# A decoder layer on one core: first transfers in halves on two queues, queries copied out of PSUM at once, values in two halves, the last factors by Ln and Exp, one result by TensorE

## The chip, the cores and the metric

The kernel runs on one core of a Trainium2 chip. The metric is the device time of one execution in microseconds (us), as the median of several runs. Engines: TensorE (PE; its weight loads are PEld in the profile), VectorE (DVE), ScalarE (ACT), GpSimd (POOL) and SyncE (SP). Transfers are issued from the queues of SP and ACT.

## The reference

One layer over 256 tokens of width 2048, batch 1, in float32. `rms_norm` has a learned gain.

```python
h = rms_norm(x, mix_pre_norm)
y = hybrid_mixer(h, ...)               # mLSTM and RWKV-7 mixers side by side, gated merge
x = x + rms_norm(y, mix_post_norm)
h, m = rms_norm(x, xattn_pre_norm), rms_norm(mem, mem_norm)
# cross_attention(h, m): 4 heads of 128, 256 memory tokens
q, (k, v) = h @ wq, split(m @ wkv)
p = softmax(q k^T / sqrt(128));  o = p v;  y = o @ wo
x = x + rms_norm(y, xattn_post_norm)
h = rms_norm(x, ffn_pre_norm)
u = conv_b + sum_j conv_w[j] * shift(h @ w_up, 2 - j)     # three taps along the tokens
gate, up = split(u)                                       # 8192 columns each
x = x + rms_norm((gelu(gate) * up) @ w_down, ffn_post_norm)
```

## The kernel before

**Products.** All big products run over pairs of numbers: each float32 operand is split into a high part, rounded to the `fp32r` format, and a low part (the rest, in the same format). One product is three matmuls: high by high, low by high, high by low. A weight chunk comes by a transfer (`raw`, three buffers; the first block's eight chunks lie in `wsm`), ACT casts it to the high part (`wh`, L361) and DVE subtracts to get the low part (`wl`, L382); both have four buffers, so the cast of chunk i waits until PE has finished chunk i - 4. `Feed` keeps this: `dma(i)`, `hi(i)`, `lo(i)` make sure that chunk i is on its way, cast, or complete.

**Blocks.** `run` takes a list of weight blocks in a fixed order. Kind `fm` gives features by tokens, kind `tm` tokens by features. A block sums over k in two or four PSUM banks (`acc` or `aux`, four of each). A block's `tail` of n means that its last n chunks are converted first, and that the products of these chunks then run bank by bank instead of chunk by chunk, so that the banks end one after another. When a block is done, its `evac` generator is given to the planner.

**The planner.** `Spread` (`side`) hands out the side work in pieces (one `next` of a generator) at each `half`, which `run` calls twice for each two-row chunk and after every second row of a tail. Each engine has a credit: a half adds 600 to DVE's and 820 to ACT's, both capped at 1200, and a piece takes what `Meter` counts for its instructions (ACT 200 + 0.83 for each element of a partition, DVE 70 + 1.04; casts and splits of the weights aren't counted, nor is work issued outside a piece). A piece of the list `bulk` goes only while both credits are above 0; the generators of the list `chains` go, in the order in which they were added, if both are above -700. `need(task)` issues pieces at once until the task is done. All this fixes the order of instructions on each engine's queue while the program is built; on the chip each engine works through its queue in order and waits on semaphores.

**The start.** x comes as eight pieces of two feature tiles (`x_load`, SP), alternating with the chunks of the first block (`w_sm`), all on SP's queue; ACT's queue takes the parameters `par` (columns 0 to 15, the first gains, and then the other 173). `pre_sm` lets PE run 8 warm-up products (`keep_warm`, 16 instructions), and `first` converts chunk 0 and x tiles 0 and 1: DVE casts the chunk's first half, ACT the second; ACT makes `hh` = x times gain (high), DVE `hl` (low).

**Cross-attention.** The order is: keys (`w_xk`), the first two of eight value chunks (`w_xv`, block `xv`), queries (`w_xq`, block `xq_`), the other six value chunks, of which the last two are the tail, and the output projection (`w_xo`). While the queries' block runs, `Residual` adds the mixer's result to x, and its statistics (`stx`) are closed by `column_of_sums` (a fold on DVE, a product `st` on PE, a power on POOL). `qx_evac` copies the queries out of PSUM (`qT`) and adds the chain of the four softmax heads, `stagger`: its first piece issues the first head's scores (`xsc`), after which `M["res"].wait(4)` gives up its turn until the statistics are done (four times at most). From then on each piece moves every live head by one stage and brings in the next: stage 1 scores and their maximum `mx`, stage 2 Exp, reciprocal and scaling (`spr`), stage 3 four transposes by PE (`xpT`) and the copy `pT`. `vx_evac` copies the values out of PSUM, scaled by the memory rows' factors (`xv`, four copies on ACT). `xo` multiplies `pT` by the values, heads 0 and 1 and then 2 and 3, and splits the result into `oT` for `w_xo`.

**The end.** The last block (`w_fd`, n = 1) has one row of k to a chunk and 64 rows; its operand `as` is split two rows at a time by `asplit` (ACT high, DVE low; one buffer for even pairs of rows, one for odd), two rows ahead of use. Its four banks are tokens 0 to 127 (banks 0 and 1, t = 0) and 128 to 255 (banks 2 and 3, t = 1). For each bank `squares` sums squares on ACT, `gain` scales on DVE; `finish(t)` gives the factor `rco` (`rstd_of`: sum and scale on DVE, power on POOL), and `result(t, c)` adds to x and issues the output transfer of a 128x512 piece. Reads of one bank by ACT and DVE follow each other.

Of the kernel before, what the change touches and what calls it, by code (L numbers as in the profile page):

```python
# [12 lines left out]
ALU = mybir.AluOpType  # L13
# [132 lines left out]
def _layer(ctx, tc, nc, d, dbg):  # L146
# [21 lines left out]
    def C(name, tag, shape=None, dt=F32):  # L168
        return mp.tile(shape or [P, S], dt, tag=tag, bufs=1, name=name)
# [13 lines left out]
    def keep_warm(n):  # L183

        q = aux("warm", [P, P])
        for _ in range(n):
            mm(q, ones.broadcast_to((P, P)), ones.broadcast_to((P, P)))
# [3 lines left out]
    xq = [x0[c // 4][:, c % 4 * 2:c % 4 * 2 + 2] for c in range(8)]  # L191
    par = cp.tile([P, NPAR], F32, name="par")
    act.dma_start(par[:, 0:16], d["par"][:, 0:16])
    act.dma_start(par[:, 16:NPAR], d["par"][:, 16:NPAR])
    con = cp.tile([P, NCON], F32, name="con")
    up = C("up", "bg0", [P, 1024])

# [9 lines left out]
    pool.memset(mhalf, -0.5)  # L207
    epsc = mhalf[:, 15:16]
    pool.memset(epsc, EPS)
    act.activation(mhalf[:, 0:1], mhalf[:, 0:1], AF.Copy)  # L210
    ones = cp.tile([P, 1], F32, name="ones")
    pool.memset(ones, 1.0)
    bones = cp.tile([P, P], F32R, name="bones")
# [112 lines left out]
    class Feed:  # L326
        def __init__(self, order):
# [3 lines left out]

            self.sm = [big(f"wsm{i}", [P, 4, 2, 384]) for i in range(2)]

        def dma(self, upto):
            while self.nd <= min(upto, len(self.src) - 1):
                s = self.src[self.nd]
                if self.nd < 8:
                    r = self.sm[self.nd // 4][:, self.nd % 4]
                else:
                    r = wp.tile(list(s.shape), F32, tag="raw", bufs=3, name="raw")  # L340
                sp.dma_start(r, s)
                self.raw[self.nd] = r
                self.nd += 1
# [74 lines left out]
    def run():  # L418
        order = visits()
        feed = Feed([(b["kind"], s) for b, c0, c1 in order for s in b["srcs"][c0:c1]])  # L420
        for c in range(8):
            x_load(c)
            feed.dma(c)
        i = 0
        pend, ring = [], []
        for b, c0, c1 in order:
# [63 lines left out]
            if nt:  # L490

                feed.lo(i + nt - 1)
                steps = []
                for s in tail:
                    w = feed.st.pop(i)
                    for kj in range(s.shape[1]):
                        steps.append((w[0][:, kj], w[1][:, kj]) + tuple(b["xs"](k)))
                        k += 1
                    i += 1
                n = len(steps)  # L500
                for g, o in enumerate(banks):
                    if b["kind"] == "tm":
                        for si, (wh, wl, xh, xl) in enumerate(steps):
                            if b is xv:
                                halves(banks, (wh, wl, xh, xl), False, si == n - 1, g)
                            else:
                                tm_products(o, g * P * 512 // b["cols"], g * 512 % b["cols"], (wh, wl, xh, xl), False,
                                            si == n - 1)
                            if si % 2:
                                side.half()  # L510
                    else:
                        turns = [(si, m) for si in range(n) for m in range(2)]
                        if g + 1 == len(banks):
                            turns.sort(key=lambda v: v[1])
                        for ti, (si, m) in enumerate(turns):
                            wh, wl, xh, xl = steps[si]
                            c = slice((g * 2 + m) * P, (g * 2 + m + 1) * P)
                            q = b["apart"] if g and m else o[:, m]
                            mm(q, wh[:, c], xh, start=ti == 0 or (bool(g and m) and si == 0), stop=False)
                            mm(q, wh[:, c], xl, start=False, stop=False)  # L520
                            mm(q, wl[:, c], xh, start=False, stop=si == n - 1)
                            if ti % 4 == 3:
                                side.half()
                    if g == 0:
                        feed.lo(i + 1)
                feed.dma(i + 4)
            if end:
                b["task"] = side.add(b["evac"](banks))
                pend.append(b["task"])

    def W(name, blk):
# [16 lines left out]

    def pre_sm(ci, feed):
        if ci == 0:  # L550
            keep_warm(8)
            feed.first()
            for c in range(1, 3):
                x_piece(c)
                feed.lo(c)
        if ci + 3 < 8:
            x_piece(ci + 3)
        else:

            for c in range((ci - 5) * 2, (ci - 5) * 2 + 2):  # L560
                st0.add(xq[c])
        if ci == 4:
            sp.dma_start(con, d["con"])
# [973 lines left out]
    def qx_evac(ps):  # L1537
# [3 lines left out]
        tasks["sm"] = side.add(stagger([softmax(h) for h in range(4)]), chain=1)  # L1541
        yield

    def vx_evac(ps):
        xv = C("xv", "bg0", [P, 2, 512])
        M["xv"] = [xv[:, t] for t in range(2)]
        for g in range(2):
            for t in range(2):
                act.activation(M["xv"][t][:, g * S:(g + 1) * S], ps[g][:, t], AF.Copy, scale=stm.rc[:, t:t + 1])
        yield  # L1550

    def stagger(gens):
# [50 lines left out]
    def xo():  # L1603
        M["oT"] = U("oT", [P, 2, 4, S], F32R)
        for h2 in range(2):
            q = aux("xo", [P, 2, S])
            for j in range(2):
                h = h2 * 2 + j
                for mt in range(2):
                    mm(q[:, j], M["xv"][mt][:, h * P:(h + 1) * P], M["pT", h][:, mt], start=(mt == 0), stop=(mt == 1))  # L1610
            split(M["oT"][:, 0, h2 * 2:h2 * 2 + 2], M["oT"][:, 1, h2 * 2:h2 * 2 + 2], q)
            yield

# [100 lines left out]
    def ax(n):  # L1714
        def xs(k):
            kk = n * 64 + k
            if kk == 58:
                side.need(fu["task"])
            if kk == 24:
                load_gain()  # L1720
            if k % 2 == 0:
                asplit(kk)
                if kk + 2 < 128 and (k < 62 or n == 0):
                    asplit(kk + 2)
            return M["as"].pop(kk)
        return xs
# [19 lines left out]
    def fd_evac(n):  # L1746

        def gen(ps):
            if n:
                z = mp.tile([P, 2, 1024], F32, tag="hT", bufs=2, name="z3")  # L1750
            else:
                z = U("z3", [P, 2, 1024])
            M["z3", n] = z

            if n == 0:
                M["ssq"], M["rco"] = small("ssq", [P, 2, 4], bufs=1), small("rco", [P, 2], bufs=1)
            ssq, rco = M["ssq"], M["rco"]

            def squares(g):
                jk = T2("jk", [P, 512])  # L1760
                act.activation(jk, ps[g], AF.Square, accum_out=ssq[:, g // 2, n * 2 + g % 2:n * 2 + g % 2 + 1])

            def gain(g):
                c = slice(g % 2 * 512, g % 2 * 512 + 512)
                dve.tensor_mul(z[:, g // 2, c], ps[g], M["gain"][:, n * 1024 + c.start:n * 1024 + c.stop])

            def finish(t):
                ss = small("sso", [P, 1], bufs=2)
                dve.tensor_reduce(ss, ssq[:, t], axis=AX.X, op=ALU.add)
                rstd_of(rco[:, t:t + 1], ss, D)  # L1770

            def result(t, c):
                f = slice(c % 2 * 512, c % 2 * 512 + 512)
                x, z_ = M["xt"][c // 2][:, t, f], M["z3", c // 2][:, t, f]
                if t and c == 1:
                    act.activation(z_, z_, AF.Copy, scale=rco[:, t:t + 1])
                    pool.tensor_add(x, x, z_)
                else:
                    dve.scalar_tensor_tensor(x, z_, rco[:, t:t + 1], x, op0=ALU.mult, op1=ALU.add)
                (act if t and c != 1 else sp).dma_start(d["out"][t, :, c * 512:c * 512 + 512], x)  # L1780

            if n == 0:
                for g in range(4):
                    squares(g)
                    gain(g)
                    yield
                return
            squares(0)
            gain(0)
            squares(1)  # L1790
            finish(0)
            gain(1)
            squares(2)
            result(0, 0)
            result(0, 1)
            gain(2)
            result(0, 2)
            squares(3)
            result(0, 3)
            finish(1)  # L1800
            gain(3)
            for c in (1, 0, 2, 3):
                result(1, c)
            yield
        return gen

    for n in range(2):
        block("tm", W("w_fd", n), ax(n), fd_evac(n), cols=1024, pool_=acc if n else aux,
              tail=3 if n else 0)
    run()  # L1810
    drain_bulk()

# [91 lines left out]
```

## Time and profile before

| | us |
|---|---|
| median of 3 runs | 1900.08 (1898.62 to 1901.8) |
| the profiled execution | 1897.44 |
| its span | 1895.7 |
| PE busy in the span | 1876.0 |
| DVE, ACT, POOL busy | 1302.0, 1013.9, 72.8 |

The profile is one execution. Its rows read: start, duration, engine, line, operation, output<-inputs, shape and count, and in brackets the idle time of the engine ahead of the row with what ended it. A row with a count is a group of the same instructions in succession. Rows of the chain of waits have start, duration and what held the chain there. Rows of the busy table have the stretch, its length, busy time and count of each engine, the granted clock, the share of the transfer engines and GB/s. The copies and sums written through the planner's meter all have line L66, all products L181: names of tiles tell them apart.

### The profile page before, as it was taken

How to read it: one execution, taken by the hardware profiler on the slowest of the kernel's cores; microseconds unless marked ns; L12 is line 12 of the kernel's file. 1: busy time of each engine (PE TensorE's matmuls, PEld its weight loads, DVE VectorE, ACT ScalarE, POOL GpSimd, SP SyncE). 2: the span in 40 equal slices, each digit the busy share in tenths (PEclk: the TensorE clock that was granted, in tenths of full speed). 3: DMA queues.
4: the chain of work that ended last, by engine and by line, in shares of the span. 5: the costliest groups of instructions: out<-in, count | busy, mean ns of one | idle time of the engine just before them, and what ended most of it. 6: DMA issues, size and time to landing. Idle time of an engine off the chain costs nothing.

```text
span 1895.7 us, 36468 instructions
## 1 busy us (share of the span) xinstructions
PE 1876.0 (99%) x15060; PEld 1788.3 (94%) x15060; DVE 1302.0 (69%) x1818; ACT 1013.9 (53%) x1464; POOL 72.8 (4%) x80
## 2 busy tenths in 40 slices
PE   9999999999999999999999999999999999999998
PEld 9999888999999999999999999999999998888886
DVE  6889786565666756678767766667766675556555
ACT  6766445555454655566555544455445455455453
POOL 0323100000000000000000000000000000000000
PEclk9999999999999999999999999999999999999999
DMA  7555554355556665445555555555565556555554
GB/s 250 181 165 186 162 176 145 112 159 158 177 177 201 225 240 183 145 162 194 189 195 191 190 197 193 195 195 190 189 197 194 196 191 214 194 192 199 190 190 154
DMA packets 97911, 352.21 MB, mean 186 GB/s; under 512 B 11024, under 2 KB 11280, under 8 KB 97360
## 3 DMA queue, kind: packets, MB, share of 16 engines
q1 hardware_dynamic: 96880, 348.73, 55.9%
q8 instruction: 118, 1.93, 0.4%
q10 hardware_dynamic: 864, 1.15, 0.2%
q14 instruction: 49, 0.40, 0.1%
HBM read 347.73 MB, written 2.10 MB: 185 GB/s over the span
## 4 chain that ended last, share of the span: by engine, by line
PE 94%; DVE 2%; ACT 2%; issue 1%; DMA 1%; POOL 0%; SPq 0%; DVEq 0%; ACTq 0%; POOLq 0%
PE fm L181 66%; PE tm L181 24%; DVE wl L382 1%; ACT wh L361 1%; PE gram L181 0%; DMA raw<-in_w_in_dram 0%; PE Y L181 0%; PE lv L181 0%; PE num L181 0%; DMA wsm<-in_w_sm_dram 0%; ACT hh L66 0%; PE zwa L181 0%; PE X L181 0%; PE gramA L181 0%; PE U L181 0%
## 5 line engine op out<-in xcount | busy, mean ns | idle before, releaser
L382 DVE TENSOR_TENSOR wl<-raw,wh 128x1024 fp32r<-128x1024 f32 x640 | 786.0, 1232 | 429.2 <-ACT wh L361 420.7
L361 ACT CAST wh<-raw 128x1024 fp32r<-128x1024 f32 x640 | 668.3, 1048 | 530.7 <-PE fm L181 354.7
L181 PE MATMUL fm<-fh,wh 128*128 128x256 f32 x2048 | 566.9, 277 | 1.4 <-ACT fh L66 1.4
L181 PE MATMUL fm<-fh,wl 128*128 128x256 f32 x2048 | 566.0, 277 | 0.0
L181 PE MATMUL fm<-fl,wh 128*128 128x256 f32 x2048 | 565.9, 277 | 0.0
L181 PEld LDWEIGHTS fm<-fh,wh 128*128 128x128 f32 x2048 | 384.7, 188 | 1.6 <-ACT fh L66 1.6
L181 PEld LDWEIGHTS fm<-fl,wh 128*128 128x128 f32 x2048 | 384.7, 188 | 0.0
L181 PEld LDWEIGHTS fm<-fh,wl 128*128 128x128 f32 x2048 | 384.6, 188 | 0.0
L181 PE MATMUL tm<-wh,as 128*128 128x512 f32 x1024 | 315.4, 389 | 0.0
L181 PE MATMUL fm<-hh,wh 128*128 128x256 f32 x1072 | 301.9, 282 | 1.5 <-ACT wh L372 1.1
L181 PE MATMUL fm<-hh,wl 128*128 128x256 f32 x1072 | 299.6, 279 | 0.7 <-DVE wl L382 0.7
L181 PE MATMUL fm<-hl,wh 128*128 128x256 f32 x1072 | 299.3, 279 | 0.0
L181 PEld LDWEIGHTS tm<-wh,as 128*128 128x128 f32 x1024 | 192.1, 188 | 40.0
L181 PEld LDWEIGHTS fm<-hh,wh 128*128 128x128 f32 x1072 | 203.2, 190 | 3.1 <-ACT hh L66 1.3
L181 PEld LDWEIGHTS fm<-hh,wl 128*128 128x128 f32 x1072 | 202.7, 189 | 1.1 <-DVE wl L382 0.9
L181 PEld LDWEIGHTS fm<-hl,wh 128*128 128x128 f32 x1072 | 202.6, 189 | 0.1
L181 PE MATMUL tm<-wl,as 128*128 128x512 f32 x512 | 199.2, 389 | 0.0
L181 PEld LDWEIGHTS tm<-wl,as 128*128 128x128 f32 x512 | 96.1, 188 | 19.8
L66 ACT CAST as<-ac 128x256 fp32r<-128x256 f32 x128 | 45.6, 404 | 112.4 <-PE tm L181 112.4
L66 DVE TENSOR_TENSOR as<-ac,as 128x256 fp32r<-128x256 f32 x128 | 48.5, 421 | 61.5 <-ACT as L66 61.5
L181 PE MATMUL fm<-mgh,wh 128*128 128x256 f32 x256 | 71.3, 279 | 0.0
L181 PE MATMUL fm<-mgl,wh 128*128 128x256 f32 x256 | 71.2, 278 | 0.0
(372 smaller groups left out, 2209.4 us busy)
## 6 DMA issues: line engine op xcount, KB each, us to landing
raw<-in_w_fu_dram SPq DMA_DIRECT2D x256, 512.0 KB, 4.3
raw<-in_w_in_dram SPq DMA_DIRECT2D x160, 512.0 KB, 3.8
raw<-in_w_fd_dram SPq DMA_DIRECT2D x128, 512.0 KB, 4.1
raw<-in_w_br_dram SPq DMA_DIRECT2D x32, 512.0 KB, 4.2
raw<-in_w_mo_dram SPq DMA_DIRECT2D x32, 512.0 KB, 4.1
raw<-in_w_xk_dram SPq DMA_DIRECT2D x8, 512.0 KB, 4.4
raw<-in_w_xv_dram SPq DMA_DIRECT2D x8, 512.0 KB, 3.9
raw<-in_w_xq_dram SPq DMA_DIRECT2D x8, 512.0 KB, 3.9
```

The lines of the kernel that those rows point to most:

```text
L66: return f(out, *a, **k)
L181: pe.matmul(out, lhsT, rhs, start=start, stop=stop, skip_group_check=True)
L361: nc.scalar.copy(wh, r)
L382: nc.vector.tensor_sub(wl, r, self.st[self.nl][0])
```

## The change

- `Feed.begin`: x tiles 0 and 1 come as two transfers of one tile each on SP; weight chunk 0 as two transfers of one half each on ACT; the other 173 parameter columns after them on ACT, and ACT's first instruction behind that. `keep_warm(10)` in place of 8.
- Queries: `need` at the end of their block issues their copies, and adds the softmax chain, at once.
- Values: `vx_half` copies a bank as soon as its part of the tail has been issued, instead of `vx_evac` after both.
- `w_fd`, n = 1: a tail of 4 in place of 3. The factor of the last norm is made by Ln and Exp on ACT: `before_last` sums and scales three of the four sums of squares on DVE, ahead of the fourth, and gives them to Ln as its bias. The table set of Ln and Exp is loaded at row 80 of the two passes.
- The result of t = 1, c = 0: PE adds x (by the identity) and z (by a diagonal of the factors) in PSUM, ACT copies it to SBUF and issues its transfer; the other three of t = 1 are DVE's and go on SP. Before, c = 1 was ACT's and POOL's.

```diff
-    act.dma_start(par[:, 16:NPAR], d["par"][:, 16:NPAR])
...
-    act.activation(mhalf[:, 0:1], mhalf[:, 0:1], AF.Copy)
...
+        def begin(self):
+
+            r = self.raw[0] = self.sm[0][:, 0]
+            for j in range(2):
+                sp.dma_start(xq[0][:, j], d["x"][:, j])
+                act.dma_start(r[:, j], self.src[0][:, j])
+            act.dma_start(par[:, 16:NPAR], d["par"][:, 16:NPAR])
+            act.activation(mhalf[:, 0:1], mhalf[:, 0:1], AF.Copy)
+            self.nd = 1
...
-        for c in range(8):
+        feed.begin()
+        for c in range(1, 8):
             x_load(c)
             feed.dma(c)
...
                     if g == 0:
                         feed.lo(i + 1)
+                    if b is xv:
+                        vx_half(banks, g)
                 feed.dma(i + 4)
             if end:
                 b["task"] = side.add(b["evac"](banks))
+                if b is xq_:
+                    side.need(b["task"])
                 pend.append(b["task"])
...
-            keep_warm(8)
+            keep_warm(10)
...
+    def vx_half(ps, g):
+        if g == 0:
+            M["xv"] = C("xv", "bg0", [P, 2, 512])
+        for t in range(2):
+            act.activation(M["xv"][:, t, g * S:(g + 1) * S], ps[g][:, t], AF.Copy, scale=stm.rc[:, t:t + 1])
+
     def vx_evac(ps):
-        xv = C("xv", "bg0", [P, 2, 512])
-        M["xv"] = [xv[:, t] for t in range(2)]
-        for g in range(2):
-            for t in range(2):
-                act.activation(M["xv"][t][:, g * S:(g + 1) * S], ps[g][:, t], AF.Copy, scale=stm.rc[:, t:t + 1])
         yield
...
+            if kk == 80:
+                tables("natural_log_exp_and_others")
...
+            def before_last(t):
+                ss = M["sso"] = small("sso", [P, 1], bufs=2)
+                dve.tensor_reduce(ss, ssq[:, t, 0:3], axis=AX.X, op=ALU.add)
+                dve.tensor_scalar(ss, ss, 1.0 / D, EPS, op0=ALU.mult, op1=ALU.add)
+
             def finish(t):
-                ss = small("sso", [P, 1], bufs=2)
-                dve.tensor_reduce(ss, ssq[:, t], axis=AX.X, op=ALU.add)
-                rstd_of(rco[:, t:t + 1], ss, D)
+                r = rco[:, t:t + 1]
+                act.activation(r, ssq[:, t, 3:4], AF.Ln, scale=1.0 / D, bias=M["sso"])
+                act.activation(r, r, AF.Exp, scale=-0.5)
...
-                if t and c == 1:
-                    act.activation(z_, z_, AF.Copy, scale=rco[:, t:t + 1])
-                    pool.tensor_add(x, x, z_)
+                if t and c == 0:
+                    diag = C("diag", "bg0", [P, P])
+                    act.activation(diag, ident, AF.Copy, scale=rco[:, t:t + 1])
+                    mm(M["sum"], diag, z_, start=False)
+                    act.copy(x, M["sum"])
                 else:
                     dve.scalar_tensor_tensor(x, z_, rco[:, t:t + 1], x, op0=ALU.mult, op1=ALU.add)
-                (act if t and c != 1 else sp).dma_start(d["out"][t, :, c * 512:c * 512 + 512], x)
+                (act if t and c == 0 else sp).dma_start(d["out"][t, :, c * 512:c * 512 + 512], x)
...
             squares(0)
+            before_last(0)
             gain(0)
             squares(1)
             finish(0)
             gain(1)
             squares(2)
+            before_last(1)
             result(0, 0)
             result(0, 1)
             gain(2)
             result(0, 2)
+            result(0, 3)
+            M["sum"] = aux("sum")
+            mm(M["sum"], ident, M["xt"][0][:, 1, 0:512], stop=False)
             squares(3)
-            result(0, 3)
             finish(1)
             gain(3)
-            for c in (1, 0, 2, 3):
+            for c in (0, 1, 2, 3):
                 result(1, c)
...
-              tail=3 if n else 0)
+              tail=4 if n else 0)
```

More of the change, by code (lines that the diff above doesn't have):

```diff
@@ L1609, in xo @@
                 for mt in range(2):
-                    mm(q[:, j], M["xv"][mt][:, h * P:(h + 1) * P], M["pT", h][:, mt], start=(mt == 0), stop=(mt == 1))
+                    mm(q[:, j], M["xv"][:, mt, h * P:(h + 1) * P], M["pT", h][:, mt], start=(mt == 0), stop=(mt == 1))
             split(M["oT"][:, 0, h2 * 2:h2 * 2 + 2], M["oT"][:, 1, h2 * 2:h2 * 2 + 2], q)
```

## Prediction

> **What bounds the kernel now.** I read the page first: busy times and the shares of the chain that ended last.
>
> ```profile
> span 1895.7 us, 36468 instructions
> PE 1876.0 (99%) x15060; PEld 1788.3 (94%) x15060; DVE 1302.0 (69%) x1818; ACT 1013.9 (53%) x1464; POOL 72.8 (4%) x80
> PE 94%; DVE 2%; ACT 2%; issue 1%; DMA 1%; POOL 0%; SPq 0%; DVEq 0%; ACTq 0%; POOLq 0%
> ```
>
> TensorE (PE) is busy for all but 19.7 us of the span, so an edit that leaves its matmuls alone can win only part of those 19.7 us: the start, the end, and a few waits. The profiled execution took 1897.44 us, 2.64 below the median of the runs (1900.08); I sum in this execution and add the sum to the median. A change of 0.2% is 3.8 us, about what a measurement of this kernel tells from none. The edits fall in three places, read in order of time.
>
> **Start.** The timeline of the first microseconds, the chain of waits of the first 60 us, PE's row at its end, and the busy table of the `fm` tiles:
>
> ```profile
> 1.17 0.46 ACTq L194 DMA_DIRECT2D par<-in_par_dram  x1
> 1.08 3.78 PE L181 MATMUL warm<-ones 128*128 128x128 f32 x16 [1.08 <-POOL ones L212]
> 4.46 0.91 ACT L66 ACTIVATE hh<-x,par 128x256 fp32r<-128x256 f32 x2 [1.30 <-DMA par<-in_par_dram]
> 5.41 0.36 DVE L368 CAST wh<-wsm 128x384 fp32r<-128x384 f32 x1 [5.41 <-DMA wsm<-in_w_sm_dram]
> 5.92 0.55 PE L181 MATMUL fm<-hh,wh 128*128 128x256 f32 x1 [1.06 <-ACT wh L372]
> 6.32 0.91 ACT L66 ACTIVATE hh<-x,par 128x256 fp32r<-128x256 f32 x2 [0.40 <-DMA x<-in_x_dram]
> 7.53 0.83 ACT L361 CAST wh<-wsm 128x768 fp32r<-128x768 f32 x1 [0.30 <-DMA wsm<-in_w_sm_dram]
> 8.39 0.96 DVE L382 TENSOR_TENSOR wl<-wsm,wh 128x768 fp32r<-128x768 f32 x1
> 2.12 5.39 DMA wsm<-in_w_sm_dram
> 30.81 7.33 DMA raw<-in_w_in_dram
> 53.52 1.22 DVE wl L382
> 54.78 0.38 PE L181 MATMUL fm<-hh,wl 128*128 128x256 f32 x1 [0.68 <-DVE wl L382]
> 6.60:10.20 3.60, 3.60 (x17) 3.51 (x17) 0.00 (x0) 0.00 (x0) 1.00 1.03 407
> 10.20:13.80 3.60, 3.60 (x34) 3.60 (x33) 0.00 (x0) 0.00 (x0) 1.00 1.05 397
> ```
>
> The first transfers become two halves of x tile 0 on SP and two halves of weight chunk 0 on ACT; the larger part of `par` goes behind them. The first product needs then only half of each, and `par`'s first columns. ACT could begin `hh` at about 4.0 to 4.46 (before it waits for `par`, which stays first on ACT's queue), so PE has its operands about 0.9 us sooner, at 5.0. The ten warm-up products run longer than that: 16 instructions took 3.78 us, the last one's own length included, so 20 end at 5.6 to 5.8. PE's first product moves from 5.92 to about 5.6 and the pause of 1.06 us closes. But PE's start isn't what the next 50 us hang on. The chain runs from the landing of weight chunk 1 (issued at 2.12, landed at 7.51) through ACT and DVE conversions and a slow weight transfer to a DVE conversion at 53.52, for which PE then waits 0.68 us. Whatever PE gains ahead of that lengthens this wait; only an earlier landing of chunk 1 counts. SP issues chunk 1 as its fourth transfer in both kernels, and the bytes ahead of it are the same by the tiles' sizes. So the nearest price is zero. ACT waited 0.40 + 0.30 us for chunk 1's data and could start 0.4 earlier, so at most 1.1 us can be won; at worst the late part of `par` (173 columns in 128 rows, 89 KB) passes ahead of chunk 1 with nothing saved before it: at the 407 GB/s of the row, 0.2 us. **Start: -0.2 (-1.1 to +0.2).**
>
> The Trainium skill speaks against a larger gain: "DMA: Bandwidth & Descriptors", section "Issuing engines are not separate DMA queues", says that transfers issued by several engines share the same engines and save only issue time; by it the term is 0 and the sum below 0.2 higher.
>
> The four DMA issues now ahead of ACT's first instruction put its table load 0.9 us later (two issues of 0.46 more), to end near 4.0: still ahead of the `par` landing that releases `hh`, so they cost nothing unless that lands sooner.
>
> **Middle: the cross-attention.** PE, ACT and DVE around the end of the value block:
>
> ```profile
> 780.80 0.28 PE L181 MATMUL fm<-qh,wl 128*128 128x256 f32 x1
> 784.82 0.63 ACT L66 ACTIVATE sq<-xr 128x512 f32<-128x512 f32 x1
> 787.70 1.07 ACT L66 COPY qT<-fm 128x512 f32<-128x512 f32 x2
> 788.11 0.50 PE L181 MATMUL st<-ones,stx 128*128 128x1 f32 x4
> 801.52 0.57 ACT L66 ACTIVATE spr<-xsc,mx,sx 128x256 f32<-128x256 f32 x1
> 802.62 1.05 ACT L361 CAST wh<-raw 128x1024 fp32r<-128x1024 f32 x1
> 802.96 0.62 DVE L66 TENSOR_SCALAR spr<-spr,psum 128x256 f32<-128x256 f32 x2
> 803.70 1.22 DVE L382 TENSOR_TENSOR wl<-raw,wh 128x1024 fp32r<-128x1024 f32 x1
> 803.71 0.60 PE L1596 MATMUL xpT<-con,spr 128*128 128x128 f32 x4
> 804.83 1.57 ACT L66 ACTIVATE xv<-tm,stm_c 128x256 f32<-128x256 f32 x4
> 805.36 3.72 PE L181 MATMUL xo<-pT,xv 128*128 128x256 f32 x16 [1.05 <-ACT xv L66]
> ```
>
> Half of the value copies now go ahead, so the wait of 1.05 us before `xo` has no ground left. That alone gives -1.05. But the queries' edit moves the softmax in the planner. Count the halves (12 products of 0.12 us) from the end of the query block at 780.9: there are twelve, 1.44 us each. Before, the query copies came at half 6 (DVE's credit had to become positive), the statistics' last steps at halves 4, 5 and 6 (784.82, the fold, 788.11), and the softmax entered the list behind the statistics. At half 7 the statistics were closed and the softmax, served after them, went on at once. Now the copies are pulled at half 0 and the softmax stands in the list ahead of the statistics, which join at half 4. DVE's credit blocks it to half 4 as it blocks the residual's last piece; at half 5 it issues the first scores; at half 7 it asks before the statistics close and goes on only at half 8. Each head comes one half later. The last half of slack returns: ACT's credit is 1200 at half 7, less 825, 1450 and 1450 with 820 back at each half, -65 at half 11, above the bound of -700, where before (the copies' 1250 charged at half 6) it was -1125 and the piece was skipped. So the last head's Exp is issued at half 11 instead of 10, its transposes after half 12 as before.
>
> What stands ahead of that Exp on ACT's queue is new: the cast (1.05) and the first value copies (two of four in 1.57, 0.8). I go through by the rows: half 10 is at about 799.1; the third head's Exp pair ends at 801.6, the cast at 802.5, value copies at 803.3, the third head's `pT` copy (128x512, as each of the two query copies that took 1.07) at 803.9. DVE does `wl` of that cast (1.22) ahead of the last head's scale of its maximum, to 804.3. Exp pair 1.2 (801.52 to the cast, and the overlap) to 805.5, reciprocal and scaling 0.8: the last transposes start at about 806.1, where PE ran out of products at 804.3; `xo` starts at 806.6 instead of 805.36. Behind it waits the output projection, fed only by `xo`. The ends: -1.05 if the softmax doesn't come later, +1.7 if the earlier transposes wait as well (0.2 to 0.3 each for the second and third head). I take the walk, since its ends are durations in rows. **Middle: +1.2 (-1.05 to +1.7).**
>
> **End.** ACT and DVE around the last four chunks, and the last instructions:
>
> ```profile
> 1876.67 0.71 ACT L66 CAST as<-ac 128x256 fp32r<-128x256 f32 x2 [1.89 <-PE tm L181]
> 1877.30 1.05 ACT L361 CAST wh<-raw 128x1024 fp32r<-128x1024 f32 x1
> 1877.11 0.76 DVE L66 TENSOR_TENSOR as<-ac,as 128x256 fp32r<-128x256 f32 x2 [1.07 <-ACT as L66]
> 1878.38 1.23 DVE L382 TENSOR_TENSOR wl<-raw,wh 128x1024 fp32r<-128x1024 f32 x1 [0.50 <-ACT wh L361]
> 1885.51 0.60 ACT L66 ACTIVATE jk<-tm 128x512 f32<-128x512 f32 x1 [1.35 <-PE tm L181]
> 1887.55 0.60 ACT L66 ACTIVATE jk<-tm 128x512 f32<-128x512 f32 x1 [1.35 <-PE tm L181]
> 1888.05 0.19 ACT L66 ACTIVATION_READ_ACCUMULATOR jk<-tm 128x1 f32 x1
> 1885.20 1.41 DVE L66 SCALAR_TENSOR_TENSOR xt<-z,rco,xt 128x512 f32<-128x512 f32 x2
> 1886.53 0.68 DVE L66 TENSOR_TENSOR z<-tm,gain 128x512 f32<-128x512 f32 x1
> 1889.46 3.08 DVE L66 SCALAR_TENSOR_TENSOR xt<-z,rco,xt 128x512 f32<-128x512 f32 x3
> 1890.26 1.74 POOL L1777 TENSOR_TENSOR xt<-xt,z 128x512 f32<-128x512 f32 x1 [0.83 <-ACT z L66]
> 1892.57 0.34 ACTq L1780 DMA_DIRECT2D out_dram<-xt  x1
> ```
>
> Banks end 2.04 us apart (1885.51 to 1887.55: nine products). A tail of four chunks makes it 2.72, twelve products: alone, the third bank ends 0.68 earlier and the fourth where it did. The tail now starts at 1876.6, and there two things come late. Chunk 63's cast takes the buffer of chunk 59, and the split of rows 126 and 127 (`as`, one buffer for each parity) that of rows 122 and 123: both are free only at 1876.6. Before, chunk 60 lay between and hid them (2.7 us); now the cast goes first (to 1877.7), then the splits; on DVE `wl` (1.23, to 1879.0) stands ahead of the low halves, so the first is there at about 1879.3. PE has only chunks 60 and 61 of bank 0 until 1878.0, one product of chunk 62, and waits: 1.1 us, for `as` from DVE. All banks end 1.1 later than planned; the third ends at 1885.9 (1885.5 before), the fourth at 1888.6 (1887.5).
>
> On DVE, `before_last(1)` stands ahead of the first results and needs the third bank's squares: DVE idles until 1885.9 + 0.75, then reduce and scale 0.3, two results 1.33, gain 0.6, two results 1.32, gain 0.6, three results. Without POOL's addition beside them (1.74; before, the three took 3.08) these take 2.1. Sum: 1885.9 + 7.0 = 1892.9, before 1892.54. The last issue moves from 1892.57 to 1892.9, and four output transfers now stand closer together. Ln and Exp replace reduce, scale and POOL's power, but DVE is still at its row of results, so they buy nothing; the diagonal, its product (two passes, about twice the 0.23 of a 256-wide one each), the copy and ACT's issue end near 1892, hidden by DVE. The table load at row 80 (1.28) is hidden: ACT waits 1.89 for PE in each pair of chunks. Ends: -0.7 if the split and cast are covered after all, +1.1 if PE's wait passes whole. **End: +0.5.**
>
> **Sum:** -0.2 + 1.2 + 0.5 = +1.5, 1898.9 in the profiled execution, **1901.6** on the median.
>
> **The rivals.** (a) Covered: neither the softmax nor the split comes late. Then -0.2 - 1.05 - 0.7 = -2.0: 1898.1. For it: rows show the 1.05 and POOL's slowing gone. Against: the list order, and the one buffer of rows 126 and 127. (b) The start pays. Busy PE from 1.08 on runs at full pace earlier: the table above has 17 products in 3.6 us and then 34, so the first chunk at full pace saves up to 1.7, of which conversions of chunk 1 (cast 0.83, then DVE 0.96 from 7.53) leave 1.3. With the other terms: 1900.5. Against: the 0.68 at 54.78. The Trainium skill, "TensorE: Matmul & The Clock Gate", Part 1, says the clock doubles after a window of about 3.4 us of steady activity, which fits the 17 and 34 (the column of the granted clock reads 1.00 in both rows and doesn't tell them apart); by it an unbroken warm-up opens the clock earlier. (c) Slower: chunk 1's weights land late, if the second queue's transfers, `par`'s short rows with them, are served ahead of it. The chain to 54.78 passes it on one to one. From +2.1 at the start (landing after 9.6) the kernel is slower by more than 0.2%; at +2.6 it is 1904.4. Against: equal bytes and issue place.
>
> **How the numbers follow.** Forecast 0.55; (a) 0.25; (b) 0.1; (c) 0.07; rest 0.03. The bounds of the terms add to -2.85 and +3.0 (1897.2 to 1903.1). Of these the low corner needs all three gains, so I end at 1898.3; at the top runs of one kernel spread by 1.6 either way, 1903.8. Faster 0.04, same 0.87 (the forecast, (a), (b)), slower 0.09 ((c) and scatter above the forecast).
>
> **What would show it.** Start: PE's first `fm` product near 5.6, chunk 1's cast still near 7.4, PE's wait for `wl` near 54.8 longer than 0.68. Middle: the `xsc` of the second head one half later, a wait of PE for `spr` of 1 to 2 us before the last `xpT`, none before `xo`. End: one wait of about 1 us for `as` from DVE at chunk 62, DVE idle about 2 us before `sso`, then without a gap to the last result. Wrong it is if PE passes these places without those waits, or if chunk 1 lands well before 7.

## The result, and the profile after

| | before | after |
|---|---|---|
| median of 12 runs each, same chip | 1899.48 (1896.98 to 1901.80) | 1903.24 (1901.55 to 1905.52) |
| ratio after to before | | 1.0020, 95% interval 1.0012 to 1.0028 |
| the profiled execution | 1897.44 | 1904.13 |
| its span | 1895.7 | 1902.3 |

The changed kernel is 3.76 us slower: 0.20%, about what the prediction named as the least that a measurement of this kernel tells from none; here the interval leaves no change out. The profile of before is of an execution 2 us below its median, that of after of one 0.9 above; so the spans differ by 6.6 us, more than the kernels do.

First the page of after. The shares of the chain that ended last hardly differ from before, but PE's busy time grew by 6.2 us (1876.0 before), nearly the whole difference of the spans, while the time in which PE stood idle grew by 0.4 only (19.7 to 20.1). So waits alone don't make up the loss: a part is products that ran longer.

```profile
span 1902.3 us, 36490 instructions
PE 1882.2 (99%) x15068; PEld 1791.5 (94%) x15068; DVE 1301.6 (68%) x1818; ACT 1016.5 (53%) x1470; POOL 70.0 (4%) x77
PE 95%; DVE 2%; ACT 1%; DMA 1%; issue 0%; POOL 0%; ACTq 0%; DVEq 0%
```

**Start.** First a row of before, the first product with the low half of chunk 1; then the timeline of after, in order of time:

```profile
10.50 0.28 PE L181 MATMUL fm<-hh,wl 128*128 128x256 f32 x1
```
```profile
5.38 0.56 PE L181 MATMUL fm<-hh,wh 128*128 128x256 f32 x1
6.31 0.51 ACT L380 CAST wh<-wsm 128x384 fp32r<-128x384 f32 x1 [1.39 <-DMA wsm<-in_w_sm_dram]
7.54 0.82 ACT L369 CAST wh<-wsm 128x768 fp32r<-128x768 f32 x1
8.39 0.96 DVE L390 TENSOR_TENSOR wl<-wsm,wh 128x768 fp32r<-128x768 f32 x1 [0.18 <-ACT wh L369]
9.40 0.39 PE L181 MATMUL fm<-hh,wl 128*128 128x256 f32 x1 [0.50 <-DVE wl L390]
47.92 0.39 PE L181 MATMUL fm<-hh,wl 128*128 128x256 f32 x1 [0.39 <-DVE wl L390]
55.03 0.38 PE L181 MATMUL fm<-hh,wl 128*128 128x256 f32 x1 [0.67 <-DVE wl L390]
```

PE begins 0.54 us sooner (5.38 instead of 5.92) and reaches its full pace sooner too, so that the product of 10.50 stands at 9.40 now, 1.1 us ahead in spite of a wait of 0.50. But the chunks don't come sooner: the second half of chunk 0, now one of two transfers on ACT's queue, keeps ACT waiting 1.39 us, so chunk 1 is cast at 7.54 (7.53 before) and its low half again starts at 8.39. PE then loses its lead, most of it in waits for later chunks (at 47.92, 51.35 and 55.03), and at 55 us the kernel is 0.25 behind. That 0.25 can't be told from none: in `e2_values` and `e4_end` below, whose start is that of before, the row of 54.78 stands at 55.64 and 55.23.

**Middle.** Here the timeline gives a clean measure: from the first product of the queries after the keys (`fm<-qh`) to the first product of the output projection (`fm<-oT`). In the first fence rows of before that the prediction didn't show (among them the second head's scores, `xsc`), in the second those of after:

```profile
758.70 0.36 PE L181 MATMUL fm<-qh,wh 128*128 128x256 f32 x1 [1.21 <-DVE kT L66]
790.86 1.02 PE L181 MATMUL xsc<-kT,qT 128*128 128x256 f32 x4
808.73 0.59 PE L181 MATMUL fm<-oT,wh 128*128 128x256 f32 x2
```
```profile
760.74 0.35 PE L181 MATMUL fm<-qh,wh 128*128 128x256 f32 x1 [1.55 <-DVE kT L66]
794.42 1.02 PE L181 MATMUL xsc<-kT,qT 128*128 128x256 f32 x4
804.39 0.85 ACT L66 ACTIVATE xv<-tm,stm_c 128x256 f32<-128x256 f32 x2
804.93 1.22 DVE L390 TENSOR_TENSOR wl<-raw,wh 128x1024 fp32r<-128x1024 f32 x1
806.32 0.56 ACT L66 ACTIVATE spr<-xsc,mx,sx 128x256 f32<-128x256 f32 x1 [0.59 <-DVE mx L66]
808.25 0.87 PE L1610 MATMUL xpT<-con,spr 128*128 128x128 f32 x4 [1.90 <-DVE spr L66]
808.92 5.10 PE L181 MATMUL xo<-pT,xv 128*128 128x256 f32 x16
813.67 0.58 PE L181 MATMUL fm<-oT,wh 128*128 128x256 f32 x2
```

50.03 us before, 52.93 after: +2.9. The second head's scores start 32.16 us into this stage before and 33.68 after, 1.52 later. The wait of `xo` for the values (1.05) is gone; in its place PE waits 1.90 for `spr` before the last head's transposes, and then `xo` takes 5.10 us instead of 3.72. The busy table of PE (its last columns: granted clock, share of the transfer engines, GB/s) says why `xo` was slow:

```profile
802.00:806.00 4.00, 3.83 (x31) 1.00 0.01 4
806.00:810.00 4.00, 2.10 (x10) 0.81 0.39 131
810.00:814.00 4.00, 4.00 (x16) 0.76 0.00 0
```

After the pause the clock was granted in part only: 0.81 and 0.76 over eight microseconds, together 1.7 us of full clock short ((0.19 + 0.24) x 4). The last transposes (0.87 for 0.60) and `xo` (5.10 for 3.72) took 1.65 us longer, about the same. The counts of the rows can't be compared, since the products differ in kind.

**End.** ACT, DVE and PE of after around the last chunks:

```profile
1881.98 1.05 ACT L369 CAST wh<-raw 128x1024 fp32r<-128x1024 f32 x1 [1.67 <-PE tm L181]
1883.07 1.23 DVE L390 TENSOR_TENSOR wl<-raw,wh 128x1024 fp32r<-128x1024 f32 x1 [1.50 <-ACT wh L369]
1884.21 0.76 DVE L66 TENSOR_TENSOR as<-ac,as 128x256 fp32r<-128x256 f32 x2
1884.68 0.50 PE L181 MATMUL tm<-wh,as 128*128 128x512 f32 x1 [0.79 <-DVE as L66]
1891.59 0.60 ACT L66 ACTIVATE jk<-tm 128x512 f32<-128x512 f32 x1 [1.47 <-PE tm L181]
1892.31 0.16 DVE L66 TENSOR_REDUCE sso<-ssq 128x1 f32<-128x3 f32 x1 [2.03 <-ACT jk L66]
1896.41 2.07 DVE L66 SCALAR_TENSOR_TENSOR xt<-z,rco,xt 128x512 f32<-128x512 f32 x3
```

PE waits 0.79 for `as`, DVE stands idle for 2.03 before `sso`. The chain of waits of after runs from PE through the third bank's squares (`jk`) to that sum, and from there without a gap through DVE's results:

```profile
1884.68 6.88 PE tm L181 x29
...
1891.59 0.70 ACT jk L66 x2
...
1892.31 0.17 DVE sso L66
...
1897.82 0.66 DVE xt L66
```

A second measure goes from the last block's first product, by the rows of the `as` products of before (first) and after, to the end of the span:

```profile
L181 PE MATMUL tm<-wh,as x1024: 389/389/397, 1539.2 to 1886.9; 128*128 128x512 f32 x171
```
```profile
L181 PE MATMUL tm<-wh,as x1024: 389/389/505, 1544.7 to 1893.7; 128*128 128x512 f32 x171
```

356.5 us before (1895.7 - 1539.2), 357.6 after: +1.1.

0.25 + 2.9 + 1.1 are 4.25 of the 6.6 us. Most of the rest arises where the change alters nothing. PE pauses 3.0 us for `so` near 361 us in both kernels; the `haT` transposes behind that pause, before and after:

```profile
363.71 1.86 PE L1240 MATMUL haT<-con,so 128*128 128x128 f32 x15 [3.00 <-DVE so L66]
```
```profile
364.12 2.90 PE L1253 MATMUL haT<-con,so 128*128 128x128 f32 x15 [3.01 <-DVE so L66]
```
```profile
366.00:368.00 2.00, 2.00 (x11) 0.50 0.00 0
```

The last row is the busy table of after: half the clock, and the transposes alone take 1.04 us longer. Between the `den` products ahead of the pause (336.4 and 336.8) and the query products (758.70 and 760.74) the traces part by 1.6 us.

### The profile page after: what moved, and what is told of

It reads as the page before. It is cut to its first block, busy times and chain, and to the rows that moved or that the text cites. A ratio compares the mean times of both kernels' runs of the same rounds, so it can differ in the third digit from the quotient of the medians.

```text
span 1902.3 us, 36490 instructions
## 1 busy us (share of the span) xinstructions
PE 1882.2 (99%) x15068; PEld 1791.5 (94%) x15068; DVE 1301.6 (68%) x1818; ACT 1016.5 (53%) x1470; POOL 70.0 (4%) x77
## 4 chain that ended last, share of the span: by engine, by line
PE 95%; DVE 2%; ACT 1%; DMA 1%; issue 0%; POOL 0%; ACTq 0%; DVEq 0%
PE fm L181 67%; PE tm L181 24%; DVE wl L390 1%; ACT wh L369 0%; PE gram L181 0%; PE Y L181 0%; DMA raw<-in_w_in_dram 0%; PE lv L181 0%; PE num L181 0%; PE xo L181 0%; DMA wsm<-in_w_sm_dram 0%; PE zwa L181 0%; PE X L181 0%; PE gramA L181 0%; PE U L181 0%
```

## Experiments

"Middle" and "end" are the two measures above, from one profiled execution; the medians are of 11 runs (`e6_warm`: 9), each against some 30 runs of the kernel before on the same chip (its medians there: 1900.27, 1900.13 and 1900.38).

| kernel | median | against before | ratio, 95% interval | middle | end |
|---|---|---|---|---|---|
| before | | | | 50.0 | 356.5 |
| after | 1903.24 | +3.76 | 1.0020, 1.0012 to 1.0028 | 52.9 | 357.6 |
| e1_queries | 1904.04 | +3.77 | 1.0016, 1.0007 to 1.0025 | 52.5 | 356.5 |
| e2_values | 1898.69 | -1.58 | 0.9988, 0.9979 to 0.9996 | 48.8 | 356.5 |
| e3_start | 1900.56 | +0.29 | 0.9998, 0.9989 to 1.0007 | 50.1 | 356.6 |
| e4_end | 1901.67 | +1.40 | 1.0007, 0.9998 to 1.0016 | 50.1 | 357.5 |
| e5_order | 1901.21 | +1.08 | 1.0016, 1.0007 to 1.0025 | 50.0 | 357.6 |
| e6_warm | 1903.98 | +3.85 | 1.0025, 1.0015 to 1.0035 | 51.1 | 357.7 |
| e7_tail3 | 1898.97 | -1.16 | 0.9997, 0.9988 to 1.0006 | 50.0 | 355.6 |
| e8_hat | 1898.90 | -1.23 | 0.9996, 0.9987 to 1.0005 | 50.4 | 356.5 |
| e9_qorder | 1900.41 | +0.03 | 1.0001, 0.9992 to 1.0010 | 49.9 | 356.5 |
| e10_tail3sum | 1900.92 | +0.54 | 1.0007, 0.9998 to 1.0016 | 50.1 | 356.9 |
| e11_best | 1896.26 | -4.12 | 0.9984, 0.9975 to 0.9993 | 49.5 | 355.5 |
| e12_bestq | 1897.02 | -3.36 | 0.9986, 0.9977 to 0.9995 | 49.9 | 355.6 |

An interval is some 1.7 us wide either way, and a difference of medians and its ratio can part by 2 us; the two measures repeat within 0.4 (middle) and 0.1 (end) where nothing was changed (`e2_values` and `e11_best`, which have the same middle, lie 0.7 apart), so they carry the finer verdicts.

**Each edit alone, on the kernel before.** Four kernels, each with one group of the hunks of the change.

```diff
 e1_queries
+                if b is xq_:
+                    side.need(b["task"])
 e2_values:  vx_half in place of the copies in vx_evac
 e3_start:   begin(), keep_warm(10)
 e4_end:     before_last, Ln and Exp, the sum by TensorE, tail=4
```

> The kernel before with the queries' edit alone. Theory 1 (place in the list): the softmax goes on one half later, the last head's Exp is issued at half 11 behind the next chunk's low half on DVE, and PE runs dry before the last transposes by about 1.9 us; all four value copies still stand behind the last pT copy, so xo starts about 2.2 to 3 us later than in the kernel before (after the last query product), +2.2 to +4 us in all, the upper end if the products after the pause run at half pace. Rival (order harmless): the early copies only free PSUM, xo starts where it did, 0 to +0.3 us.

> The kernel before with the values' edit alone. Theory 1: the softmax keeps its halves, the first two value copies and the last two are done before the last pT copy or beside it, PE's wait of 1.05 us before xo is gone: -1.0 us. Rival (the copies stand in front of the last head's Exp or pT on ACT): the wait moves to the last transposes, 0 to +0.5 us.

> The kernel before with the start alone (first transfers by tiles on two queues, parameters behind, ten warm-up products). Theory 1 (the conversion chain from chunk 1 is what counts): PE's first fm product at 5.4 instead of 5.9, full pace from about 6.2, but chunk 1's cast again at 7.5 and the wait for wl near 55 at 55.0: 0 to +0.3 us. Rival (PE's start counts): PE keeps 0.5 to 1.3 us of it past 55 us, -0.5 to -1.3 us.

> The kernel before with the end alone (tail of 4, Ln and Exp, one result by PE, table load at row 80). Theory 1 (one buffer of rows 126 and 127): PE waits 0.8 us for as at chunk 62, DVE waits for the third bank's squares before the first results, +1.2 us at the end. Rival (the bank's earlier end pays): PE doesn't wait, the last DVE result ends 0.7 us earlier, -0.5 to -0.7 us. A third: the table load at row 80 or what follows costs PE 1.3 us in the middle of the block; the shift would then show before the last eight rows.

The four differences of medians add to +3.9, the change's own is +3.76 (the ratios add to 1.0009, with their four intervals wide enough to hold 1.0020): no interaction of the parts can be told by the medians. The start alone went as its theory had it, but for one row: chunk 1 was cast at 7.91 (7.5 expected). PE's wait near 55 us ended at 54.89 (55.0 expected). The queries' edit carries the loss. Its timeline has the wait of after; the values, copied late in this kernel, make `xo` wait as well, and here `xo` runs at full pace:

```profile
805.84 0.63 PE L1598 MATMUL xpT<-con,spr 128*128 128x128 f32 x4 [1.90 <-DVE spr L66]
807.53 3.72 PE L181 MATMUL xo<-pT,xv 128*128 128x256 f32 x16 [1.05 <-ACT xv L66]
```

The values' edit alone does what it should: with the softmax in its old order `xo` waits for nothing (timeline of e2_values).

```profile
805.38 3.67 PE L181 MATMUL xo<-pT,xv 128*128 128x256 f32 x16
```

**Is it the copies or the order?** `e5_order` is the changed kernel, `e9_qorder` the queries' edit on the kernel before, both with this line in the planner, so that the softmax is served behind the statistics as it was:

```diff
-        for s in list(self.chains):
+        for s in sorted(self.chains, key=lambda s: s["gen"].gi_code.co_name == "stagger"):
```

> The changed kernel, with one difference: the planner serves the softmax generator after the other chains, as it stood before; the query copies stay early and no instruction is added or removed. Theory (the place in the planner's list delays every head by one half): the second head's scores return to half 7, the last head's transposes run inside the tail, PE's wait of 1.90 us for spr goes, and xo starts with at most the small wait for the fourth pT. Against the changed kernel -1.5 to -3.5 us, so 0 to +2 against the kernel before. Rival (the early query copies cost by themselves, for instance by shifting the conversions around them): PE still waits near 1.9 us before the last transposes, and the time stays 3 to 4 us above the kernel before.

> The kernel before with the queries' edit and the softmax generator served last, as in the run that put this order into the changed kernel. Theory (the place in the planner's list is the edit's cost): PE's wait before the last transposes falls below 1.1 us instead of 1.90, the time lies 0 to 1.5 us above the kernel before and 2 to 4 below the kernel with the queries' edit alone. Rival (copying early costs by itself): 2.5 to 4 us above the kernel before, as the queries' edit alone.

```profile
806.56 0.63 PE L1598 MATMUL xpT<-con,spr 128*128 128x128 f32 x4 [1.04 <-DVE spr L66]
808.45 3.62 PE L181 MATMUL xo<-pT,xv 128*128 128x256 f32 x16
```

That is the timeline of e9_qorder. The wait falls from 1.90 to 1.04, the last products of the value block run between these transposes and `xo`, and the cost of the queries' edit goes from +3.77 to +0.03 (52.5 to 49.9 in the middle): on the kernel before, the place in the list was its whole cost, to within the 1.7 us of an interval. In `e5_order` the middle returns to 50.0 too; its time is less clear, for seven of its runs lie at 1900.2 to 1902.6 and four at 1904.2 to 1906.0, so that its median says +1.1 (the end's share) and its ratio +3.0. My expectation that the wait would go altogether was wrong, it stayed at 1.03. The heads aren't late any more: counted from the first query product (761.82 in e9_qorder), the second head's scores start at 32.13 (32.16 before, 33.68 in after) and the last transposes at 44.74 us (45.01 before, 47.51 in after). These transposes now stand ahead of the last value products on PE's queue, where they stood behind them before, and PE waits for `spr` there instead of waiting for `xv` at `xo`. So the early copies, in the old order too, take from the values' edit a part of what it wins: with both the middle is 50.0 and 49.9 (`e5_order`, `e12_bestq`), with the values' edit and no early copies 48.8 and 49.5 (`e2_values`, `e11_best`).

**Does the pause cost more than its length?** `e6_warm` puts 16 matmul instructions into PE's pause before the last head's transposes in the changed kernel, `e8_hat` 20 into that before `haT` in the kernel before; the transposes overwrite what they write.

```diff
 e6_warm
+        if h == 3:
+            for _ in range(8):
+                mm(q[:, 0, 0:P], ones.broadcast_to((P, P)), ones.broadcast_to((P, P)))
 e8_hat
+            if k4 == 0:
+                for _ in range(10):
+                    mm(qs[0][:, 0, 0:P], ones.broadcast_to((P, P)), ones.broadcast_to((P, P)))
```

> The changed kernel with 16 more matmul instructions (about 0.128 us each, 2.05 us), which write a bank that the last head's transposes overwrite; they stand ahead of these transposes on PE's queue and run in its pause of 1.90 us. Theory (a pause makes the products behind it run at half pace): the last transposes take 0.6 instead of 0.87 us, xo 3.7 instead of 5.1 us, the time falls by 1.0 to 1.5 us against the changed kernel. Rival (xo is slow for another reason, such as the values' copies beside it, or the half pace comes from before the pause): xo keeps 5.1 us, the time is the same or up to 0.3 us more, by what the warm products run over the pause.

> The kernel before with 20 more matmul instructions (2.6 us) in PE's pause of 3.0 us near 361 us (the wait for so ahead of the haT transposes); they write a bank that the first transposes overwrite. Theory (that pause leaves the products behind it at half pace in some executions and not in others, 1.6 us between them): the haT group takes 1.9 us in each profile, the median falls by 0.6 to 1.6 us against the kernel before. Rival (the pace behind that pause does not depend on PE being idle): the median stays within 0.5 us, and a profile may still show the haT group at 2.9 us.

In the profile of `e6_warm` `xo` takes 3.62 us and the middle is 1.8 shorter than in after, as the theory has it, but the median isn't lower (+3.85 against +3.76, on two chips; the two intervals leave room for a saving of 1.4 us). The half pace behind this pause isn't a cost of every execution, for the profile of `e1_queries`, with the same pause of 1.90, was without it. Its mean price stays open; the expected saving of 1.0 to 1.5 us wasn't seen. In `e8_hat` the wait for `so` shrinks from 3.0 to 0.8 us, and `haT` runs at full pace (timeline):

```profile
360.02 2.39 PE L181 MATMUL haT<-ones 128*128 128x128 f32 x20
363.30 1.86 PE L1243 MATMUL haT<-con,so 128*128 128x128 f32 x15 [0.78 <-DVE so L66]
```

Its median lies 1.23 below, within its interval of no change, but its 11 runs spread over 2.4 us (1897.78 to 1900.13), the 31 of the kernel before beside them over 7.5. That the filled pause is the reason isn't shown: the runs of `e2_values` and `e7_tail3`, which don't fill it, spread over 3.1 and 3.2, those of the two kernels at the end of this section, which do, over 3.3 and 3.9.

**Which part of the end?** Both have the new end with a tail of three; `e7_tail3` also moves the sum.

```diff
 e7_tail3 (e10_tail3sum leaves before_last(1) where the change put it)
             squares(2)
-            before_last(1)
             result(0, 0)
             result(0, 1)
+            before_last(1)
```

> The kernel before with the new end (Ln and Exp, result by TensorE, new order of results), but with its tail of three chunks, and with the last sum ahead of the fourth bank moved behind the first two results. Theory (the tail of four costs its wait for the split of rows 126 and 127, 0.8 to 1.1 us, and the sum placed ahead of the first results makes VectorE idle 2 us): no wait for as, no idle 2 us, the time is 1.0 to 1.8 us below the kernel before and 2.4 to 3.2 below the kernel with the whole new end alone. Rival (Ln, Exp and the product cost by themselves): between 0 and +1.5 us against the kernel before.

> The kernel before with the new end and its order as in the change, but a tail of three chunks: the sum ahead of the fourth bank stays in front of the first results. It parts the two suspects of the end. If the tail's wait for as (0.79 us) is the cost: within 0.5 us of the kernel that moved the sum as well, so -1.2 to 0 against the kernel before. If the sum's place (VectorE idle for 2 us) is the cost: +0.8 to +1.5 against the kernel before, as with the whole new end.

By the end measure the tail of four costs 0.7 (357.6 to 356.9), the place of the sum 1.3 (356.9 to 355.6): two causes, neither alone. The medians follow (+1.40, +0.54, -1.16), but by steps that they alone couldn't tell from none. In the timeline of e7_tail3 DVE has the first two results behind it when the third bank's sum is due, and begins the last three right after the fourth bank's scaling:

```profile
1887.16 1.41 DVE L66 SCALAR_TENSOR_TENSOR xt<-z,rco,xt 128x512 f32<-128x512 f32 x2
1888.60 0.16 DVE L66 TENSOR_REDUCE sso<-ssq 128x1 f32<-128x3 f32 x1
1889.92 0.60 ACT L66 ACTIVATE jk<-tm 128x512 f32<-128x512 f32 x1 [1.35 <-PE tm L181]
1890.78 0.68 DVE L66 TENSOR_TENSOR z<-tm,gain 128x512 f32<-128x512 f32 x1
1891.38 2.07 DVE L66 SCALAR_TENSOR_TENSOR xt<-z,rco,xt 128x512 f32<-128x512 f32 x3
```

**A version that beats both.** Values half by half, the end of `e7_tail3`, the products in the `haT` pause; `e12_bestq` adds the queries' edit with the order line.

> The parts that paid, together: values half by half, the new end with a tail of three and the sum behind the first two results, and 20 warm-up instructions in the pause of 3.0 us near 361 us; no edit of the start or the queries. If the parts add up (-1.6, -0.4 to -1.2, -1.2): 3.0 to 4.0 us below the kernel before, with the same narrow spread as the run with the warm-up products alone. Rival (they share a cause or spread): -1.0 to -2.0.

> The same as the run without the queries' edit, and with the queries copied early with the softmax served last. Theory (in the old order the early copies cost nothing): within 0.8 us of that run. Rival (the early copies cost beside the order): 1 to 2.5 us above it, with a wait of PE near 1.0 us before the last transposes.

`e11_best` is 4.12 us below the kernel before, by the ratio 3.0 (1.3 to 4.8): that is about what the three parts add to (4.0 by their medians), and it beats both kernels. The early copies bring nothing: `e12_bestq` is 0.76 above it, too little to tell, and waits 1.04 before the last transposes. The narrow spread that was expected with the filled pause didn't come (3.3 us).

## Why the prediction was right or wrong

The forecast was 1901.6 within 1898.3 to 1903.8, +1.5 on the median; measured were 1903.24 and +3.76 (2.3 to 5.3 by the ratio's interval). That the time lies inside the range is partly luck: the change is more than the +3.0 to which the bounds of the terms add, and what kept the time inside was the 0.7 added on top for scatter and a median of before that came out 0.6 lower here (1899.48 for 1900.08). The mechanisms of the middle and the end came as forecast, but the trace puts each term above its forecast: 0.25, 2.9 and 1.1 where -0.2, 1.2 and 0.5 stood, 4.25 in place of 1.5. The middle's lies above the top of its bounds (1.7).

- **Start (-0.2, in the trace +0.25, e3_start +0.29; none of these is told from nothing).** "Only an earlier landing of chunk 1 counts" held: PE was 1.1 us ahead at 9.40 and behind at 55 us. The prediction had the wait at 55 us grow; it stayed (0.67 for 0.68), and the lead went into four waits for `wl` instead, 1.9 us in all where there was one of 0.7. Rival (b), that the start pays, was right that PE would reach its full pace sooner (from about 6.4, where it took until about 10.3), but nothing of it was left at 55 us in the traces of after and `e3_start`; the runs of `e3_start` (2.1 us less to 1.3 more) wouldn't rule it out by themselves. The step that failed is ACT's: it was to have chunk 1 up to 0.4 sooner, but its wait moved to chunk 0's second half (1.39).
- **Middle (+1.2, in the trace +2.9, e1_queries and e2_values together +2.2).** The walk through the planner was right nearly row by row: the second head's scores came 1.52 later, one half. Less the 2.04 us that after is behind at the query products, the last transposes begin at 806.21 (forecast 806.1) and `xo` at 806.88 (806.6), 1.5 later than before; the value copies, the cast and `wl` stand ahead of the last Exp and scaling as listed. That the place in the list is the cause, which the walk took from the code alone, is shown by e9_qorder. What was mis-sized lies behind the walk's end: it took the products after the pause at their old pace, and in the traced execution they took 1.4 us more (5.10 for 3.72); with the 1.5 that is the 2.9. How often the medians pay that is open (e6_warm).
- **End (+0.5, in the trace +1.1, e4_end +1.40).** PE's wait for `as` was 0.79 (forecast 1.1), DVE's idle time 2.03 (about 2). Less the 5.5 us that after is behind at the last block's first product, DVE's last result ends at 1892.98, where the forecast had 1892.9. The missing 0.66 comes behind it: from DVE's last result to the end of the span 3.82 us pass (1898.48 to 1902.3) where there were 3.16 (1892.54 to 1895.7). It is the last transfer's own time: issued at 1898.51, it lands 2.8 us later, where the last one of before, issued at 1892.57, took 2.1. The prediction said that the output transfers stand closer together and priced that at nothing; whether it is this or their place on SP's queue wasn't tried. With the sum behind two results and a tail of three (`e7_tail3`) the end is 0.9 shorter than before, although a last transfer takes 2.8 there too. This isn't shown to be the work of Ln and Exp: the last three results alone save 1.0 (2.07 for 3.08), with POOL's addition no longer beside them, and the new way of the factor wasn't tried by itself.
- **Rival (a), covered,** fell with the two waits, for `spr` and for `as`. **Rival (c)** did not come: chunk 1 was cast at 7.54 to 7.91 in the four profiles with the new start, at 7.40 to 7.99 in the ten with the old one. That a late chunk 1 passes to 55 us one to one isn't borne out: in `e3_start` it was cast 0.38 later than before, and PE's row there came 0.11 later.
- Not thought of: that one profile can lie 2 us below its median and another 0.9 above, in part by the clock behind a pause that the change doesn't touch.

## What to carry to other kernels

Work that is issued earlier by hand also changes its place in a planner's list, and the items it overtakes may be those it depends on: follow the list, half by half, before counting the gain, and move the place back (one line here, 2.6 us of the middle in the traces, 3.7 between the medians). At the end of a kernel look for what the engine that ends last does while it waits for a sum: results that need nothing more go ahead of it. And measure a small edit between two rows of its own stage: over the whole span one execution differs from the next by more than the edit is worth.

## What the runs showed of the hardware

The clock after a pause of PE differs between executions of the same program. Behind the pause of 3.0 us near 361 us, eight of the eleven profiles without filler have a stretch granted at 0.50, three (before, e1_queries, e2_values) have 1.00 throughout. Behind the pause for `hsl` near 207 us, which lasts 1.42 to 1.96 us in the fourteen profiles, two show it (e5_order, e6_warm): here e5_order, a row of PE and one of the busy table, and the same of e9_qorder, whose pause is as long and leaves the clock at 1.00.

```profile
209.90 0.39 PE L181 MATMUL bon<-hsl,bones 128*128 128x256 f32 x1 [1.96 <-DVE hsl L66]
```
```profile
210.00:213.00 3.00, 3.00 (x18) 0.66 0.75 213
```
```profile
206.78 0.39 PE L181 MATMUL bon<-hsl,bones 128*128 128x256 f32 x1 [1.95 <-DVE hsl L66]
```
```profile
210.00:213.00 3.00, 3.00 (x28) 1.00 0.67 247
```

The pause of 1.2 to 1.6 us for `kT` near 760 us never showed it. The Trainium skill, "TensorE: Matmul & The Clock Gate", Part 1, has the clock fall to half after an idle window of about 3.4 us. The half agrees with the rows; the length doesn't hold as a threshold here, since 1.88 us were enough in one execution and 3.0 too little in three.

A good part of the spread of the runs goes with this. Of the 97 runs of the kernel before, by the mean granted clock of the run: 17 at 0.999 took 1898.5 us in the mean, 41 at 0.998 1899.9, 28 at 0.997 1900.8, 11 at 0.996 1902.0.
